# Choosing 16 experts among 96 sums instead of 256, and making the gate rows of four tokens by two operations

## The chip, the cores and the metric

One core of a Trainium2 chip runs the whole program. Its engines work side by side and wait for each other by semaphores: TensorE (PE in the profile; PEld is its weight load), VectorE (DVE), ScalarE (ACT), GpSimd (POOL) and SyncE (SP, which here only issues DMAs). The metric is the time of one execution on the device, in microseconds (us). The kernel before takes 3847.57 us, the median of three runs (3845.66 to 3850.11).

## The reference, cut to what matters

Two layers work on 512 latent and 256 context tokens with 1024 features. Each layer has a mixer and then PEER, a retrieval among 16384 = 128 x 128 experts. For each token and each of 8 heads, PEER takes the 16 best of 128 scores twice, adds every one of the first 16 to every one of the second 16, and takes the 16 best of these 256 sums:

```
sv, si = lax.top_k(s, PEER_TOPK)
cand = (sv[:, :, 0, :, None] + sv[:, :, 1, None, :]).reshape(PEER_BLOCK, PEER_HEADS, kk)
cidx = (si[:, :, 0, :, None] * PEER_NKEYS + si[:, :, 1, None, :]).reshape(PEER_BLOCK, PEER_HEADS, kk)
top_s, pos = lax.top_k(cand, PEER_TOPK)
eidx = jnp.take_along_axis(cidx, pos, axis=-1)
gate = jax.nn.softmax(top_s, axis=-1)
act = jax.nn.gelu(jnp.einsum('nd,nhkd->nhk', hb, u_tab[eidx]).astype(F32), approximate=False)
w = (gate * act).astype(hb.dtype)
return jnp.einsum('nhk,nhkd->nd', w, v_tab[eidx])
```

Both lists of 16 are sorted, largest first. The sum of number a of the first list and number b of the second has at least (a+1)(b+1)-1 others that are no smaller, so it can be among the 16 best only where (a+1)(b+1) is at most 16.

## The kernel before, in words

The time goes to PEER. Tokens come in tiles of 128. In layer 0 tiles 0 to 3 are *dense*: all 16384 experts are computed for them and multiplied by gates that are zero except at the chosen ones. Tiles 4 and 5 are *gathered*: the rows of the chosen experts alone are fetched, one row per token, by indirect DMAs. In layer 1 tiles 0 to 2 are dense and tile 3 is gathered. Each layer has two stages.

- **The u stage.** `u_chunk` loads 128 experts of the table u (`c_raw`), splits them into two parts (`c_hi` by ACT, `c_lo` by DVE, line 298) and multiplies both with the dense tokens: 24 matmuls into `ups`. There are 128 such chunks per layer, and 16 chunks of the query weights of the same form between them. ACT applies the gelu and the result goes to memory.
- **The v stage.** For each chunk POOL multiplies that result with the gates (`w`, line 1059), ACT and DVE split the product and the table v, and PE multiplies them into `res`.

Around the u chunks stands the other work of PEER, which DVE carries above all:

- `scores` takes the 16 best of 128 scores (lines 716 to 721).
- `select` takes the 16 best of the 256 sums: four heads are added at a time (`cand`, line 737), each head is searched by five DVE instructions (lines 743 to 748), the position in the list is taken apart into its two numbers (lines 754 and 756), and the indices are looked up (`eq`, lines 758 to 768).
- `build` makes the gates of a dense tile, 32 steps of four tokens. ACT makes one factor `o1`, of each token (lines 805 and 806). DVE makes the other, `o2`: one instruction per token (line 809) compares a row of 0 to 127 with the token's second index and multiplies by its gate. PE multiplies the two (`gps`), and ACT copies the result to `stage` (line 814).
- `gather` fetches one row per token for one of 128 choices (POOL's indirect DMA, line 667). DVE then makes its product with the token (line 671, table u) or adds it, weighted, to `g_acc` (line 675, table v). A gathered tile has 256 such steps.

A planner sets the order. After each chunk `back` advances three clocks, of PE, DVE and the DMAs, by the costs in `COST`. Pieces of `select` and `build` for the dense tiles are placed evenly over the chunks. While DVE's clock is behind PE's, further pieces of the early work are issued: the choice for the gathered tiles and rows to gather, at 1.15 us each, up to `GU` of them (340 in layer 0, 160 in layer 1). Rows that the u stage did not gather are spread over the v stage. Each engine then runs its instructions in the order so laid down.

Of the kernel before, what the change touches and what calls it, by code (L numbers as in the profile page):

```python
# [9 lines left out]
F32 = mybir.dt.float32  # L10
F32R = mybir.dt.float32r
BF16 = mybir.dt.bfloat16
# [6 lines left out]
P = 128  # L19
# [35 lines left out]
COST = {"build": (1.03, .73, .85), "gather": (1.15, 1.46, 0), "cand": (1.14, 0, 0), "top": (1.0, 0, 0), "top2": (.67, 0, 0),  # L55
# [6 lines left out]
class Tracked:  # L62
    """an engine, with its latest instruction"""
# [13 lines left out]
def kernel(tc, a, out):  # L77
# [52 lines left out]
    class Operand:  # L130
        """The two exact parts of what a phase multiplies with, features on partitions"""

        class Cols:
            """columns in more than one tile"""
# [19 lines left out]
        def fill(self, b, src):  # L154
            """block b of the features"""
            for c0, c1 in self.bounds:
                split(self.hi[:, b, c0:c1], self.lo[:, b, c0:c1], src[:, c0:c1])

        def freed(self):
            """a token tile's room twice in the last columns, which nothing reads any more"""  # L160
            c0, c1 = self.bounds[1]
            return [self.pool.tile([P, KB, c1 - c0], F32, name=f"{self.name}{z}f", tag=f"{self.name}{z}{c0}")[:, :, :P]
                    for z in "hl"]
# [17 lines left out]
    def mod_piece(l, j, w, pp, tag="small", bufs=2, after=None, queue=SP):  # L181
        """512 columns of the modulation, four column groups of the array side by side"""
# [43 lines left out]
    def like(v, shape_of):  # L226
        """a row of features as the blocks that another one comes in"""
        return v if len(shape_of.shape) == len(v.shape) else v.rearrange("p (b n) -> p b n", n=P)

    def resid_norm(y, xsrc, gb, wp, bufs=2, tp=None, tmp=None, xb=2, cut=1):  # L230
        """alpha x + gate y of one token tile, its mean and the inverse of its deviation"""
# [19 lines left out]
    def resid_ln(y, xsrc, dst, gb, lg, lb, wp, xo=None, bufs=2, tp=None, xb=2, cut=1):  # L251
        """LN(alpha x + gate y) of one token tile, in dst"""
# [9 lines left out]
    def normed(y, xsrc, gb, wp, bufs=2, tp=None, tmp=None, xb=2, cut=1):  # L262
        """the same without the gain and the bias of the norm, which what follows applies on its own"""
# [12 lines left out]
    def behind_norm():  # L276
        """what may wait until the latest norm is through"""
# [8 lines left out]
    def fold(i, l, sh, sc):  # L286
        """gain and bias of norm i together with the modulation that follows it"""
# [15 lines left out]
    def mm_chunk(ps, wh, wl, hh, hl, n):  # L303
        """ps[m, tok] = w^T h over the KB blocks of the contraction."""
# [16 lines left out]
    def turn(hf, ps, xt, t, scale, shift, all_act=False, b0=0):  # L321
        """x scale + shift with features on partitions"""
# [17 lines left out]
    def peer_hT(l, t, xt, mod, gt, wp, wide, n):  # L340
        """operand of the PEER sub-layer, in steps; a tile whose experts are gathered keeps it whole, in both layouts"""
# [13 lines left out]
    def proj_rows(l, wp, pp, small):  # L355
        """what proj_out multiplies and adds along the features"""
# [9 lines left out]
    def proj_out(op, l, wh, wl, xsrc, gt, wp, rows, wops, turned, nb, lags):  # L366
        """x <- LN(alpha x + gate * (mix @ w_out)) and what PEER takes of it, in steps; says which tile comes next"""
# [60 lines left out]
    LATE = [(0, 10), (0, 11)] + [(1, j) for j in range(4)]  # L428

    def mixer0(gt):  # L430
        with ExitStack() as es:
# [37 lines left out]
            def taps(g, up):  # L469
                """the taps of one group of channels, by the vector engine or by the scalar engine and GpSimd"""  # L470
# [12 lines left out]
            def taps_pe(g, uh, ul):  # L483
                """the taps of one group of channels, by the tensor engine with diagonal matrices"""
# [112 lines left out]
            # layer norm over the channels, which lie on the partitions  # L597
# [49 lines left out]
    def peer(op, l, gt, xdst):  # L647
# [45 lines left out]
        with ExitStack() as es:  # L693
# [29 lines left out]
            chosen = {}  # L723

            def select(t):
# [6 lines left out]
                sh4 = [P, HB, TOPK, TOPK]  # L732
                ijg = wp.tile([P, 3, HEADS, TOPK], F32, name=f"ijg{z}", bufs=1)
                for h0 in (0, HB):
                    hs = slice(h0, h0 + HB)
                    cand = wp.tile(sh4, F32, name=f"cand{z}", bufs=1)
                    V.tensor_tensor(cand, v4[:, hs, 0, :].unsqueeze(3).to_broadcast(sh4),
                                    v4[:, hs, 1, :].unsqueeze(2).to_broadcast(sh4), op=OP.add)
                    yield "cand"
                    for h in range(HB):  # L740
                        src = cand[:, h].rearrange("p a b -> p (a b)")
                        s2 = wp.tile([P, 256], F32, name=f"c2{z}", bufs=1)
# [8 lines left out]
                    for s in range(2):  # L751
                        pi = wp.tile([P, HB, TOPK], U32, name=f"pi{z}", bufs=2)
                        if s == 0:
                            V.tensor_scalar(pi, pos[:, hs], 4, None, op0=OP.logical_shift_right)
                        else:
                            V.tensor_scalar(pi, pos[:, hs], 15, None, op0=OP.bitwise_and)
# [34 lines left out]
                chosen[t] = tr  # L791
                yield "gates"

            def build(t):
                """the gates of a dense tile, by expert and token"""
                tr = chosen.pop(t)
                W8 = 4
                for g in range(P // TG):
                    stg = wp.tile([P, P, TG], F32, name="stage", bufs=2)
                    for b in range(TG // W8):  # L800
# [6 lines left out]
                        for i in range(W8):  # L807
                            n1 = slice(n0 + i, n0 + i + 1)
                            V.tensor_scalar(o2[:, i], iota, tr[:, 1, n1], tr[:, 2, n1],
                                            op0=OP.is_equal, op1=OP.mult)  # L810
# [7 lines left out]
            def merged(gens):  # L818
                """generators side by side, each as far along as the other; gens: (generator, its cost)"""
# [875 lines left out]
```

## Time and profile before

| | before |
|---|---|
| runs, median (lowest to highest) | 3847.57 us (3845.66 to 3850.11) |
| profiled execution, first to last instruction | 3842.2 us |
| PE busy | 3659.1 us |
| DVE busy | 3152.0 us |
| ACT busy | 1836.8 us |
| POOL busy | 1722.5 us |
| u stage of layer 0, from chunk 17 on | about 447 to 1390 us of the span |
| v stage of layer 0 | about 1390 to 2070 us |
| u stage of layer 1 | about 2525 to 3290 us |
| v stage of layer 1 | about 3290 to 3830 us |

The busy share of PE counts a matmul from its start to a modelled end. Several overlap, so a busy PE can still be slower than it could be. How much work it did is read from the number of matmuls in a stretch. For DVE, an instruction's duration includes some 0.07 us in which the next one already runs, so the engine's busy time is less than the sum of its durations.

### The profile page before, as it was taken

The page shows a single profiled execution, that of the slowest core. Times are in us where ns is not written, and L with a number is a line of the kernel's source. Part 1 is how long each engine was busy: PE and PEld are TensorE (multiplying, and loading weights), DVE is VectorE, ACT ScalarE, POOL GpSimd, SP SyncE. Part 2 cuts the span into 40 slices and gives each one's busy share as a digit, 9 for nine tenths or more (in the row PEclk, how much of TensorE's full clock was granted, in tenths as well). Part 3 has the DMA queues.
Part 4 walks back from the last instruction along what each step waited for, and adds up shares of the span by engine and source line. Part 5 has one row for each costly group of instructions (what it writes and reads, how often), then busy time and mean ns, then how long its engine had stood idle before and what let it go on. Part 6 is the DMA issues. An engine that isn't in the chain of part 4 may idle for free. (4 is left out here: it accounts for less than half of the span.)

```text
span 3842.2 us, 57154 instructions
## 1 busy us (share of the span) xinstructions
PE 3659.1 (95%) x20375; PEld 3162.6 (82%) x20375; DVE 3152.0 (82%) x6412; ACT 1836.8 (48%) x3234; POOL 1722.5 (45%) x1225
## 2 busy tenths in 40 slices
PE   7789999999999999999998999899999999999998
PEld 5567877788888778888887888789999999887876
DVE  4877899999999868998886616688999987688778
ACT  4243322378888832322224424533358988333332
POOL 4300055444445557887871203103422223577764
PEclk9899999999999999999999999899999999999999
DMA  5225598889999999999993330157978989888885
GB/s 232 88 91 198 180 326 307 302 319 355 366 344 356 373 338 355 359 367 367 356 342 136 127 127 4 66 192 276 314 263 320 314 290 342 300 318 321 324 314 197
DMA packets 377149, 1044.00 MB, mean 272 GB/s; under 512 B 32288, under 2 KB 171936, under 8 KB 346656
## 3 DMA queue, kind: packets, MB, share of 16 engines
q1 hardware_dynamic: 262960, 619.56, 44.1%
q0 software_dynamic: 113760, 420.53, 30.4%
q8 instruction: 160, 2.62, 0.3%
q14 instruction: 125, 1.02, 0.1%
q10 hardware_dynamic: 144, 0.26, 0.0%
HBM read 915.98 MB, written 124.26 MB: 271 GB/s over the span
## 5 line engine op out<-in xcount | busy, mean ns | idle before, releaser
L667 POOL DMA_INDIRECT g_row<-in_peer_u_dram,g_idx x384 | 529.1, 1378 | 788.5 <-DVE g_row L671 397.0
L667 POOL DMA_INDIRECT g_row<-in_peer_v_dram,g_idx x384 | 576.5, 1501 | 308.0 <-DVE g_acc L675 188.9
L297 ACT CAST c_hi<-c_raw 128x1024 fp32r<-128x1024 f32 x304 | 318.2, 1047 | 593.3 <-PE ups L69 484.4
L298 DVE TENSOR_TENSOR v_lo<-v_raw,v_hi 128x1024 fp32r<-128x1024 f32 x256 | 409.7, 1600 | 214.8 <-ACT v_hi L297 214.5
L297 ACT CAST v_hi<-v_raw 128x1024 fp32r<-128x1024 f32 x256 | 269.3, 1052 | 656.5 <-DMA v_raw<-in_peer_v_dram 380.0
L1059 POOL TENSOR_TENSOR w<-ag,gg 128x512 f32<-128x512 f32 (+1 forms) x256 | 455.2, 1778 | 278.7 <-DVE w_lo L298 234.2
L69 PE MATMUL res<-v_hi,w_hi 128*128 128x512 f32 x1792 | 556.1, 391 | 12.6 <-ACT w_hi L297 12.6
L69 PE MATMUL res<-v_lo,w_hi 128*128 128x512 f32 x1792 | 555.3, 390 | 1.1
L69 PE MATMUL res<-v_hi,w_lo 128*128 128x512 f32 x1792 | 554.5, 390 | 0.0
L675 DVE SCALAR_TENSOR_TENSOR g_acc<-g_row,g_act,g_acc 128x1024 f32<-128x1024 f32 x381 | 533.2, 1399 | 2.2
L298 DVE TENSOR_TENSOR c_lo<-c_raw,c_hi 128x1024 fp32r<-128x1024 f32 x304 | 373.3, 1229 | 147.0 <-ACT c_hi L297 143.9
L671 DVE SCALAR_TENSOR_TENSOR g_row<-g_row,g_h 128x1024 f32<-128x1024 f32 x384 | 488.1, 1288 | 6.2 <-DMA g_row<-in_peer_u_dram,g_idx 6.0
L69 PE MATMUL ups<-opah,c_hi 128*128 128x512 f32 x1152 | 458.5, 398 | 4.9 <-ACT c_hi L297 4.9
L69 PE MATMUL ups<-opah,c_lo 128*128 128x512 f32 x1152 | 453.4, 394 | 9.7 <-DVE c_lo L298 9.4
L69 PE MATMUL ups<-opal,c_hi 128*128 128x512 f32 x1152 | 451.3, 392 | 0.0
L69 PEld LDWEIGHTS res<-v_hi,w_hi 128*128 128x128 f32 x1792 | 336.6, 188 | 85.9 <-ACT w_hi L297 16.7
L69 PEld LDWEIGHTS res<-v_lo,w_hi 128*128 128x128 f32 x1792 | 336.3, 188 | 75.0 <-DVE v_lo L298 5.6
L69 PE MATMUL ups<-opch,c_hi 128*128 128x384 f32 x1152 | 393.7, 342 | 3.7 <-ACT c_hi L297 3.7
L69 PEld LDWEIGHTS res<-v_hi,w_lo 128*128 128x128 f32 x1792 | 336.2, 188 | 71.1 <-DVE w_lo L298 2.0
L69 PE MATMUL ups<-opch,c_lo 128*128 128x384 f32 x1152 | 387.8, 337 | 3.6 <-DVE c_lo L298 3.6
L69 PE MATMUL ups<-opcl,c_hi 128*128 128x384 f32 x1152 | 386.7, 336 | 0.0
L805 ACT ACTIVATE o<-iota,ijT 128x128 f32<-128x128 f32 x896 | 293.0, 403 | 0.2
(469 smaller groups left out, 6699.8 us busy)
## 6 DMA issues: line engine op xcount, KB each, us to landing
c_raw<-in_uT_dram SPq DMA_DIRECT2D x256, 512.0 KB, 6.1
v_raw<-in_peer_v_dram SPq DMA_DIRECT2D x128, 1024.0 KB, 7.7
G_d<-stage SPq DMA_DIRECT2D x56, 1024.0 KB, 7.8
c_raw<-in_peer_wq_dram SPq DMA_DIRECT2D x64, 512.0 KB, 4.9
gg<-G_d SPq DMA_DIRECT2D x64, 512.0 KB, 9.8
A_d<-at SPq DMA_DIRECT2D x120, 256.0 KB, 6.4
ag<-A_d SPq DMA_DIRECT2D x30, 1024.0 KB, 10.9
gg<-G_d SPq DMA_DIRECT2D x64, 384.0 KB, 8.9
```

Source lines behind the costliest of these rows:

```text
L69: self.last = self.engine.matmul(*args, **kw)
L297: copied[0] = S.copy(hi, src)
L298: return V.tensor_tensor(lo, src, hi.bitcast(F32), op=OP.subtract)
L667: G.indirect_dma_start(out=row, out_offset=None, in_=a[f"peer_{'uv'[tab]}{l}"], in_offset=bass.IndirectOffsetOnAxis(ap=idx[i][:, s:s + 1], ...
L671: V.scalar_tensor_tensor(row, row, 1.0, h, op0=OP.mult, op1=OP.mult, accum_out=w)
L675: V.scalar_tensor_tensor(acc, row, w, acc, op0=OP.mult, op1=OP.add)
L805: S.activation(o1[:, i], iota, AF.Abs, bias=tr[:, 0, n0 + i:n0 + i + 1])
L1059: G.tensor_tensor(w.rearrange("p (t m) -> p t m", m=TG), ag[:, i], gg[:, :, (c + i) % GG, :], op=OP.mult)
```

## The change

The sums that cannot be among the 16 best are left out. `cand` now has 96 places per head, made by three additions: 2 x 16 sums, 2 x 8 and 12 x 4. Each search looks at 96 places. A position no longer splits by a shift and a mask alone, and eight small instructions take it apart where two did. For the gates, the indices of a tile are kept in bf16 as well (`jT`), and `o2` of four tokens is made by two DVE instructions: a comparison of 512 elements in bf16 (`oe`), and a multiplication by the gates that writes 512 elements of 4 bytes. The multiplication runs over the tokens innermost, and the four tokens' rows lie 512 bytes apart in `o2`. So each element is written 512 bytes from the one before it. Three costs in the planner's table are lowered (`cand`, `top`, `top2`); those of `build`, `gather` and `eq` stay. The rest of the diff removes comments, and is left out here.

```diff
-COST = {"build": (1.03, .73, .85), "gather": (1.15, 1.46, 0), "cand": (1.14, 0, 0), "top": (1.0, 0, 0), "top2": (.67, 0, 0),
+COST = {"build": (1.03, .73, .85), "gather": (1.15, 1.46, 0), "cand": (.55, 0, 0), "top": (.7, 0, 0), "top2": (.45, 0, 0),
...
+            CAND = ((0, 0, 2, 16), (32, 2, 2, 8), (48, 4, 12, 4))
+            fifteen = wp.tile([P, TOPK], U32, name="fifteen")
+            V.memset(fifteen, 15)
+            W8 = 4
+            iotar = wp.tile([P, P, W8], BF16, name="iotar")
+            V.tensor_copy(iotar, iota.unsqueeze(2).to_broadcast([P, P, W8]))
...
-                    cand = wp.tile(sh4, F32, name=f"cand{z}", bufs=1)
-                    V.tensor_tensor(cand, v4[:, hs, 0, :].unsqueeze(3).to_broadcast(sh4),
-                                    v4[:, hs, 1, :].unsqueeze(2).to_broadcast(sh4), op=OP.add)
+                    cand = wp.tile([P, HB, 96], F32, name=f"cand{z}", bufs=1)
+                    for p0, a0, na, nb in CAND:
+                        shc = [P, HB, na, nb]
+                        V.tensor_tensor(cand[:, :, p0:p0 + na * nb].rearrange("p h (a b) -> p h a b", b=nb),
+                                        v4[:, hs, 0, a0:a0 + na].unsqueeze(3).to_broadcast(shc),
+                                        v4[:, hs, 1, :nb].unsqueeze(2).to_broadcast(shc), op=OP.add)
...
-                        src = cand[:, h].rearrange("p a b -> p (a b)")
-                        s2 = wp.tile([P, 256], F32, name=f"c2{z}", bufs=1)
+                        src = cand[:, h]
+                        s2 = wp.tile([P, 96], F32, name=f"c2{z}", bufs=1)
...
-                            V.tensor_scalar(pi, pos[:, hs], 4, None, op0=OP.logical_shift_right)
-                        else:
-                            V.tensor_scalar(pi, pos[:, hs], 15, None, op0=OP.bitwise_and)
+                    V.tensor_scalar(pb, pos[:, hs], 32, None, op0=OP.is_ge)
+                    V.scalar_tensor_tensor(pb, pos[:, hs], 48, pb, op0=OP.is_ge, op1=OP.add)
+                    V.tensor_scalar(pa, pb, -1.0, 4.0, op0=OP.mult, op1=OP.add)
+                    V.tensor_tensor(pa, pos[:, hs], pa, op=OP.logical_shift_right)
+                    V.tensor_tensor(pm, fifteen.unsqueeze(1).to_broadcast(sh3), pb, op=OP.logical_shift_right)
+                    V.tensor_tensor(pm, pos[:, hs], pm, op=OP.bitwise_and)
+                    V.scalar_tensor_tensor(pb, pb, 2.0, pb, op0=OP.mult, op1=OP.mult)
+                    V.tensor_tensor(pa, pa, pb, op=OP.subtract)
+                    for pi in (pa, pm):
...
+                jb = wp.tile([P, P], BF16, name="jT", bufs=2)
+                S.copy(jb, pt[:, 1])
...
-                        for i in range(W8):
-                            n1 = slice(n0 + i, n0 + i + 1)
-                            V.tensor_scalar(o2[:, i], iota, tr[:, 1, n1], tr[:, 2, n1],
-                                            op0=OP.is_equal, op1=OP.mult)
+                        sh, nb = [P, P, W8], slice(n0, n0 + W8)
+                        oe = wp.tile(sh, BF16, name="oe", bufs=2)
+                        V.tensor_tensor(oe, iotar, jb[:, nb].unsqueeze(1).to_broadcast(sh), op=OP.is_equal)
+                        V.tensor_tensor(o2.rearrange("p n c -> p c n"), oe, tr[:, 2, nb].unsqueeze(1).to_broadcast(sh),
+                                        op=OP.mult)
```

The first place is DVE's order behind the 106th `c_lo`, in the u stage of layer 0, while the gates of one dense tile are made and the next tile's choice runs. Before it reads so (`o` with its buffer's number is `o2`, one row of four instructions per step; x4 and x2 are counts):

```order
L298 TENSOR_TENSOR c_lo<-c_raw,c_hi 128x1024
L675 SCALAR_TENSOR_TENSOR g_acc<-g_row,g_act,g_acc 128x1024
L743 MAX topd<-candd 128x8
L675 SCALAR_TENSOR_TENSOR g_acc<-g_row,g_act,g_acc 128x1024
L744 MAX_INDEX posd<-topd,candd 128x8
L745 MATCH_REPLACE c2d<-topd,candd 128x256
L809 TENSOR_SCALAR o_9167<-iota,ijT 128x128 x4
L809 TENSOR_SCALAR o_9184<-iota,ijT 128x128 x4
L675 SCALAR_TENSOR_TENSOR g_acc<-g_row,g_act,g_acc 128x1024
```

And now, behind the same `c_lo` (`oe` and `o` are the two operations of a step):

```order
L298 TENSOR_TENSOR c_lo<-c_raw,c_hi 128x1024
L824 TENSOR_TENSOR oe<-iotar,jT 128x512
L757 MAX topd<-c2d 128x8
L825 TENSOR_TENSOR o_9222<-oe,ijT 128x128x4
L758 MAX_INDEX posd<-topd,c2d 128x8
L824 TENSOR_TENSOR oe<-iotar,jT 128x512
L675 SCALAR_TENSOR_TENSOR g_acc<-g_row,g_act,g_acc 128x1024 x3
```

Before, each gate step is one run of four instructions. Now its two operations stand apart with other work between them, and the second operation of the last step shown comes only behind the next `c_lo`. Three gathered rows stand in both pieces. The second place is POOL's queue where the u stage of layer 0 ends and the products of the v stage (`w`) begin, before:

```order
L667 DMA g_row<-in_peer_u_dram,g_idx_2679 128x1024 x128
L667 DMA g_row<-in_peer_v_dram,g_idx_2679 128x1024 x128
L667 DMA g_row<-in_peer_u_dram,g_idx_2680 128x1024 x67
L1059 TENSOR_TENSOR w<-ag,gg 128x512 x3
L667 DMA g_row<-in_peer_u_dram,g_idx_2680 128x1024
```

And now:

```order
L667 DMA g_row<-in_peer_u_dram,g_idx_2679 128x1024 x128
L667 DMA g_row<-in_peer_v_dram,g_idx_2679 128x1024 x128
L667 DMA g_row<-in_peer_u_dram,g_idx_2680 128x1024 x95
L1075 TENSOR_TENSOR w<-ag,gg 128x512 x3
L667 DMA g_row<-in_peer_u_dram,g_idx_2680 128x1024
```

So 28 gathered rows move from the v stage into the u stage of layer 0 (323 stood ahead of the first `w`, now 351), and 6 in layer 1. Counted along DVE's order between the same `c_lo` (the numbers of the chunks run through the program), with the time at which that part ran before:

| chunks | time before, us | gathered rows, before / now | gate steps, before / now | heads searched, before / now |
|---|---|---|---|---|
| 17 to 77, layer 0 | 447 to 818 | 122 / 135 | 6 / 5 | 21 / 18.5 |
| 77 to 137, layer 0 | 818 to 1238 | 147 / 162 | 93 / 92.5 | 22.5 / 22 |
| 137 to 153, layer 0 | 1238 to 1364 | 44 / 44 | 29 / 30 | 0 / 0 |
| 221 to 277, layer 1 | 2833 to 3122 | 63 / 71 | 62 / 59 | 17 / 17 |
| 277 to 301, layer 1 | 3122 to 3266 | 33 / 22 | 34 / 37 | 0 / 0 |

## Rows read from the trace of the kernel before

**Rows 1.** Busy time by stretch: us, each engine's busy (x), granted clock, DMA

```profile
core 0: us, PE busy (x) PEld busy (x) DVE busy (x) ACT busy (x) POOL busy (x), PEclk, DMA share, GB/s
447.00:744.00 297.00, 284.74 (x1284) 229.62 (x1283) 289.84 (x926) 85.67 (x108) 145.12 (x106) 0.99 0.82 296
818.00:1238.00 420.00, 415.34 (x2195) 354.50 (x2194) 415.91 (x883) 351.56 (x698) 206.01 (x148) 1.00 0.97 357
1400.00:2060.00 660.00, 660.00 (x2914) 546.64 (x2913) 563.82 (x530) 197.72 (x251) 509.96 (x311) 1.00 0.91 343
2833.00:3122.00 289.00, 289.00 (x1841) 288.51 (x1840) 261.50 (x641) 256.56 (x501) 75.09 (x63) 1.00 0.88 308
3122.00:3266.00 144.00, 137.17 (x855) 132.45 (x854) 108.70 (x216) 125.47 (x258) 46.48 (x33) 0.99 0.90 317
1238.00:1338.00 100.00, 93.01 (x517) 77.05 (x516) 91.00 (x209) 95.22 (x202) 57.60 (x39) 1.00 0.99 367
```

**Rows 2.** The same stretch of layer 0, matmuls of ups, then of gps

```profile
818.00:1238.00 420.00, 345.06 (x1444) 266.04 (x1442) 35.57 (x61) 1.00 0.97 357
818.00:1238.00 420.00, 93.36 (x742) 92.02 (x743) 97.46 (x92) 1.00 0.97 357
```

**Rows 3.** The chain of waits: start us, us, what

```profile
2868.28 1.78 PE gps L69 x16
```

**Rows 4.** Waits, 420 to 800 us, then 1238 to 1338: us in total, times, longest

```profile
PEld ups L69 <- DVE c_lo L298: 13.8, 14, 5.9
PEld gps L69 <- ACT o L806: 12.9, 14, 1.3
```

**Rows 5.** DVE in order of time from 818 us: start, us, what

```profile
824.19 1.22 DVE L298 TENSOR_TENSOR c_lo<-c_raw,c_hi 128x1024 fp32r<-128x1024 f32 x1
825.33 1.11 DVE L809 TENSOR_SCALAR o<-iota,ijT 128x128 f32<-128x128 f32 x4
826.35 0.42 DVE L747 MAX8 topd<-c2d 128x8 f32<-128x256 f32 x1
```

**Rows 6.** DVE by line, 818 to 1238 us: xcount | busy us, mean ns | idle

```profile
L675 DVE SCALAR_TENSOR_TENSOR g_acc<-g_row,g_act,g_acc 128x1024 f32<-128x1024 f32 x127 | 163.0, 1283 | 0.1
L809 DVE TENSOR_SCALAR o<-iota,ijT 128x128 f32<-128x128 f32 x372 | 107.0, 365 | 0.0
L743 DVE MAX8 topd<-candd 128x8 f32<-128x256 f32 x22 | 9.4, 426 | 0.0
L737 DVE TENSOR_TENSOR candd<-sv 128x1024 f32<-128x1024 f32 x5 | 6.1, 1226 | 0.0
L754 DVE TENSOR_SCALAR pid<-posd 128x64 uint32<-128x64 uint32 x6 | 1.3, 213 | 0.0
```

**Rows 7.** The whole span by line and shape: DVE, then ACT

```profile
L716 DVE MAX8 sv<-scps 128x8 f32<-128x128 f32 x160 | 47.0, 294 | 17.4 <-PE scps L69 17.1
L1251 DVE TENSOR_TENSOR ML<-mB,mx 128x4 f32<-128x4 f32 x12 | 1.7, 159 | 0.0
L1171 DVE TENSOR_TENSOR rny<-rny,rope 128x128 f32<-128x128 f32 x4 | 1.2, 289 | 0.6 <-POOL rsw L1169 0.6
L298 DVE TENSOR_TENSOR opal<-csq,opah 128x512 fp32r<-128x512 f32 x4 | 2.8, 691 | 3.1 <-ACT opah L297 3.0
L766 DVE TENSOR_TENSOR eqd<-eqd 128x512 bf16<-128x512 bf16 x28 | 11.8, 424 | 0.1
L768 DVE TENSOR_TENSOR ijgd<-eqd 128x64 f32<-128x64 bf16 x28 | 7.9, 286 | 0.1
L814 ACT COPY stage<-gps 128x512 f32<-128x512 f32 x224 | 237.1, 1069 | 0.7
L212 ACT COPY gb<-gps 128x512 f32<-128x512 f32 x6 | 3.5, 585 | 8.5 <-PE gps L69 8.5
```

**Rows 8.** DVE by line, 2833 to 3122 us: the gate rows and a gathered row

```profile
L671 DVE SCALAR_TENSOR_TENSOR g_row<-g_row,g_h 128x1024 f32<-128x1024 f32 x63 | 76.2, 1215 | 0.0
L809 DVE TENSOR_SCALAR o<-iota,ijT 128x128 f32<-128x128 f32 x248 | 69.1, 348 | 0.5 <-PE gps L69 0.5
```

More of the change, by code (lines that the diff above doesn't have):

```diff
@@ L732, in select @@
                 sh4 = [P, HB, TOPK, TOPK]
+                sh3 = [P, HB, TOPK]
                 ijg = wp.tile([P, 3, HEADS, TOPK], F32, name=f"ijg{z}", bufs=1)
@@ L750, in select @@
                     eqs = []
-                    for s in range(2):
-                        pi = wp.tile([P, HB, TOPK], U32, name=f"pi{z}", bufs=2)
-                        if s == 0:
-                            V.tensor_scalar(pi, pos[:, hs], 4, None, op0=OP.logical_shift_right)
-                        else:
-                            V.tensor_scalar(pi, pos[:, hs], 15, None, op0=OP.bitwise_and)
+                    pb, pa, pm = (wp.tile(sh3, U32, name=f"p{y}{z}", bufs=2) for y in "bam")
+                    V.tensor_scalar(pb, pos[:, hs], 32, None, op0=OP.is_ge)
[7 more added lines that the diff above has]
+                    for pi in (pa, pm):
                         eq = wp.tile(sh4, BF16, name=f"eq{z}", bufs=2)
@@ L790, in select @@
                 S.copy(tr, pt)
-                chosen[t] = tr
+                jb = wp.tile([P, P], BF16, name="jT", bufs=2)
+                S.copy(jb, pt[:, 1])
+                chosen[t] = tr, jb
                 yield "gates"
             def build(t):
-                tr = chosen.pop(t)
-                W8 = 4
+                tr, jb = chosen.pop(t)
                 for g in range(P // TG):
```

## The prediction

> **What bounds the kernel now.** I read the busy times by stretch first, then DVE's groups by line inside the stretches that the change touches, then the waits, and last the durations of like instructions over the whole span.
>
> By stretch, PE looks full everywhere, so the reader is to count matmuls instead. In the v stage of layer 0 PE is busy for all of 660 us and starts 2914 matmuls of 512 columns, 0.2265 us each [rows 1]. That is PE's full rate, since the granted clock is 1.00. In the stretch 818 to 1238 us there are 1444 matmuls of `ups` at that rate, 327 us, and 742 of `gps` [rows 2], which run 16 in 1.78 us where PE is the chain [rows 3], so 82 us more. PE needs 409 of the 420 us. DVE is busy for 415.9 of the same 420 us [rows 1]. So DVE sets this stretch, with PE 11 us behind as the next bound. From 447 to 744 us it is DVE too (289.8 of 297), and there PE does wait for `c_lo` [rows 4]. In layer 1, from 2833 to 3122 us, PE has no idle time and DVE is busy for 261.5 of 289, so 27.5 us are free on it [rows 1]. At the ends of both u stages, where gate steps come without a choice beside them, ACT is the fullest engine (95.2 of 100 us from 1238 to 1338) and PE waits for ACT's factor [rows 1, 4]. So the change is decided on DVE, stretch by stretch, by what goes and what comes.
>
> **What one piece costs.** An instruction's start to the next one's start is about 0.07 us less than its duration: a `c_lo` of 1.22 us is followed after 1.14, four gate rows of 1.11 after 1.02 [rows 5]. I take 0.07 off everything.
>
> *A gate step before:* 372 instructions, 93 steps, take 107.0 us [rows 6], so 1.15 a step, 1.08 net.
>
> *A gate step now,* first operation: 512 elements, all bf16. The nearest row is an addition of 512 bf16 elements at 424 ns; the dearest that it could be is 691, as 512 elements of 4 bytes take [rows 7]. I take 0.42, as the type is the same. Second operation: 512 elements with a result of 4 bytes, so 691 ns at least. But each element is written 512 bytes from the last one. No DVE row of before writes so. ACT's copy to `stage` writes 512 elements 64 bytes apart and takes 1069 ns; its copy of the same size from the same kind of tile to neighbouring places takes 585 [rows 7]: 0.94 ns more for each element. And DVE has one instruction that reads its 64 elements 32 bytes apart (line 768): 286 ns, where 4 elements take 159 and 128 take 289, so that 64 should take about 222 [rows 7]: 1.0 ns more for each. Both say that an element on a place of its own costs about one more nanosecond. For 512 that is 0.53 us, and 691 becomes about 1.22 us. The bounds are 0.69 (nothing more) and 1.26 (ACT's ratio 1.83). I take 1.22, since both rows with such a step show it. A step is then 0.42 + 1.22 - 0.14 = 1.50 us net, 0.42 more than before.
>
> The Trainium skill describes how such places are read (Advanced Engine Details and Errata, SBUF Cachelines): accesses that each fall in another line of 16 bytes are slowed, and two in a line are needed for full speed. It names no price; the two rows agree with it. Against it stands another page (VectorE: DVE Perf Modes, Mode 1x (REGULAR) — the baseline), by which this mode makes one result a cycle, odd strides included. By the first the sum below stands, by the second it is that of the first rival.
>
> *A searched head:* five instructions over 256 elements at about 426 ns become five over 96. 128 elements take 294 [rows 6, 7], so 96 should take 0.26, an estimate by the slope between the two. That saves 0.16 each, 0.8 us a head. *The additions:* one of 1226 ns becomes three of 128, 64 and 192 elements, 0.29 + 0.22 + 0.36 by the rows at 4 and 128 elements [rows 6, 7], 0.5 us less net for four heads. *The positions:* eight instructions where two were. At 213 ns each [rows 6] that is 0.14 net, 0.8 us more for four heads; zero to 0.3 each would make 0 to 2 us of it. *A gathered row:* 1.283 us with table v [rows 6], 1.215 with table u [rows 8], 1.21 and 1.15 net. ACT's extra copy of the indices, seven in all, and the two constants made once are nothing beside this: ACT is busy for 1837 of 3842 us.
>
> **The sum.** The planner does not keep what the choice saves. It charges less for a choice, finds its DVE clock behind PE's sooner, and puts gathered rows there: 28 in layer 0 and 6 in layer 1 move ahead, with their DMAs on POOL's queue.
>
> - 447 to 818 us: 13 rows more (+15), 18.5 searched heads cheaper (-15) and 2.5 fewer (-5), additions and positions about +1, one gate step fewer but five dearer (+1). I take -3.
> - 818 to 1238 us: 93 gate steps (+39), 15 rows (+18), 22 heads (-18), five additions (-2.5), six times the positions (+5). Sum +42. DVE has 4 us left that are waits, and PE's 11 us are already inside the 420, so all of it is on the path: +42.
> - 1238 to 1364 us: 30 steps (+13) and as many rows as before. ACT is the bound, but in its first 100 us DVE has 91 busy and would have 103. I take +5.
> - 2833 to 3122 us: a step was 69.1/62 - 0.07 = 1.05 us net [rows 8], so 59 steps at 1.50 make +24; 8 rows (+9), 17 heads (-14), additions and positions +2. DVE rises by 21 to 283 of 289. PE's chunks hide most of it; for the crowding I take +3, and 0 to 10 as bounds.
> - 3122 to 3266 us: 37 steps in place of 34 (+20), 11 rows fewer (-13); DVE 116 of 144 with ACT in front. +2.
> - v stages: 28 and 6 rows fewer to add up. In layer 0 PE is full for all 660 us, so nothing comes back; layer 1 has too few rows to matter. 0. This is the point of the case: rows are moved from where DVE's work was free to where it is the bound.
>
> Together +49. The profiled execution spans 3842.2 us, the median of the runs is 3847.57, so 5.4 us lie around the span or between executions. The span becomes 3891 and the time about 3897 us.
>
> **The rivals.**
>
> *The write is not slowed* (second operation 0.69 us). A step is 0.97 net, 0.11 less than before. Then 818 to 1238 us gets -7 in all, the first stretch -3, the ends about -1: 3837 us. For it speaks that no DVE row writes with such a step; against it, both rows that have one. PE's floor of 409 us forbids more than -11 there. This is the case on the faster side, and it decides for any second operation below about 0.75 us.
>
> *The same, but the DMAs eat it.* In that stretch the queues are busy 0.97 at 357 GB/s [rows 1], and 15 rows of 512 KB are 7.9 MB, 5% of what it moves. If it gets no longer, `c_raw` comes late by about what is won: 3847 us, no change.
>
> *Half the price.* The write costs about 0.95 us: 0.27 less a step, -25 in the second stretch and -3 around it: 3870 us. For it speaks only that DVE's one row is a read with two such inputs.
>
> *The comparison runs at one element a cycle* (0.69 us). 0.27 more a step: +25, then +8 at the end of layer 0, and in layer 1 DVE passes PE (283 + 16 of 289), +10 and +3: about 3943 us. Against it, the bf16 addition of as many elements takes 424 ns [rows 7].
>
> *The choice saves nothing*, since the planner refills it: that is not a rival but part of the sum, and the rows counted in the order show it.
>
> **How the numbers follow.** The forecast (3880 to 3925) has 0.63, half the price (3855 to 3880) 0.12, the slow comparison (3925 to 3955) 0.10, no change 0.07, faster 0.08. The predicted time is the forecast's, 3897. The range that leaves two in ten out is 3858 to 3935: outside lie no change, faster and about half of the slow comparison. The likeliest case alone has 3880 to 3925. A measurement of this kernel tells about 0.2%, 7.7 us, from no change. By that, slower has 0.85, no change 0.07 and faster 0.08.
>
> **What would show it.** In the profile after: the second operation of a gate step near 1.22 us and the comparison near 0.42; a search of 96 places near 0.26; DVE busy all through the u stage of layer 0, which ends some 45 us later, and PE waiting for `c_lo` between 818 and 1238 us of before, with fewer matmuls in 100 us; the v stage of layer 0 as long as before. It is wrong if the second operation takes about 0.7 us, or if that stretch gets no longer although DVE has more to do in it.

## The result: slower, by half of what was forecast

| | before | after |
|---|---|---|
| runs on one chip, median (lowest to highest) | 3850.11 us (3845.66 to 3855.41), 5 runs | 3873.78 us (3862.14 to 3875.51), 5 runs |
| profiled execution, first to last instruction | 3842.2 us | 3873.7 us |
| ratio of the times, 95% interval | 1 | 1.0056 [1.0041, 1.0071] |

The changed kernel is 0.56% slower, 24 us, where 49 were forecast. The time lies in the range that was given, and the direction is right; but it lies below the likeliest case (3880 to 3925), within the bounds of the rival at half the price. The two spans differ by 31.5 us, more than the medians. The profiled execution of after took 3875.51 us, 1.8 us more than its span and the slowest of its five. With the same 1.8 us the one of before took about 3844, below all of its runs. So between stretches of the two traces some 5 to 8 us in all are scatter.

The busy times of after by stretch, cut at the same `c_lo` as those of before [rows 1] (whose first row ends earlier, at 744 us); the columns are stretch, length, each engine's busy time and instructions, granted clock, DMA share and GB/s:

```profile
core 0: us, PE busy (x) PEld busy (x) DVE busy (x) ACT busy (x) POOL busy (x), PEclk, DMA share, GB/s
446.00:819.00 373.00, 359.03 (x1614) 290.99 (x1613) 360.12 (x1142) 124.41 (x173) 197.94 (x140) 0.98 0.86 312
819.00:1261.00 442.00, 421.32 (x2184) 354.91 (x2182) 437.38 (x775) 354.80 (x703) 267.45 (x162) 0.99 0.97 354
1261.00:1392.00 131.00, 122.30 (x654) 102.65 (x654) 109.09 (x167) 104.73 (x215) 65.79 (x46) 1.00 1.00 370
1423.00:2083.00 660.00, 660.00 (x2913) 546.69 (x2912) 499.96 (x477) 196.61 (x250) 471.55 (x284) 1.00 0.89 324
2868.00:3156.00 288.00, 286.57 (x1816) 285.70 (x1815) 273.36 (x568) 250.41 (x488) 99.39 (x72) 1.00 0.90 322
3156.00:3303.00 147.00, 139.45 (x887) 135.13 (x886) 105.69 (x127) 133.34 (x277) 34.54 (x23) 1.00 0.82 289
```

The second row carries the result. The same 60 chunks took 420 us before and take 442, with as many matmuls (2184, 2195 before), and DVE is busy for 437 of the 442. Of the other stretches the end of that stage got 5 us longer (131 against 126 from 1238 to 1364 us of before), the first one 2 (373 against 371), layer 1's last 3. In 660 us of the v stage of layer 0 PE starts as many matmuls as before (2913, 2914 before), while DVE's busy time there fell from 564 to 500 us: the rows that left it gave nothing back. From the first matmul of `res` to the last that stage takes 711 us, and took 710.

The ends of these stretches are starts of `c_lo` on DVE, which can run ahead of PE. Counted on PE instead, from the start of one matmul of `ups` to the start of another, the same two in both kernels, the busy stretch takes 420 us before and 448 after, and the end of that stage 126 and 124. So the two together got 25 to 27 us longer, and how this splits between them depends on where the border is set.

DVE by line in the stretch 819 to 1261 us of after, to be laid beside [rows 6]; behind the count stand busy us, mean ns, and idle time:

```profile
L675 DVE SCALAR_TENSOR_TENSOR g_acc<-g_row,g_act,g_acc 128x1024 f32<-128x1024 f32 x121 | 154.3, 1275 | 2.7 <-DMA g_row<-in_peer_v_dram,g_idx 1.8
L825 DVE TENSOR_TENSOR o<-oe,ijT 128x512 f32<-128x512 bf16 x92 | 98.4, 1083 | 0.0
...
L671 DVE SCALAR_TENSOR_TENSOR g_row<-g_row,g_h 128x1024 f32<-128x1024 f32 x41 | 48.9, 1222 | 1.7 <-DMA g_row<-in_peer_u_dram,g_idx 1.7
L824 DVE TENSOR_TENSOR oe<-iotar,jT 128x512 bf16<-128x512 bf16 x93 | 37.5, 415 | 0.0
...
L753 DVE MAX8 topd<-candd 128x8 f32<-128x96 f32 x22 | 5.4, 245 | 0.0
...
L746 DVE TENSOR_TENSOR candd<-sv 128x128 f32<-128x128 f32 (+2 forms) x15 | 3.8, 288 | 0.0
```

The comparison (L824) takes 0.415 us and a search 0.245, as forecast. The second operation (L825) takes 1.083, where 1.22 was taken. There are 162 rows in place of 147, as counted in the order. How much of the 1.08 us the engine is really held shows in DVE's order of time (start us, us, what):

```profile
899.72 1.07 DVE L825 TENSOR_TENSOR o<-oe,ijT 128x512 f32<-128x512 bf16 x1
900.63 1.21 DVE L298 TENSOR_TENSOR c_lo<-c_raw,c_hi 128x1024 fp32r<-128x1024 f32 x1
901.77 0.40 DVE L824 TENSOR_TENSOR oe<-iotar,jT 128x512 bf16<-128x512 bf16 x1
902.10 0.24 DVE L757 MAX8 topd<-c2d 128x8 f32<-128x96 f32 x1
902.27 1.10 DVE L825 TENSOR_TENSOR o<-oe,ijT 128x512 f32<-128x512 bf16 x1
903.22 0.06 DVE L758 MATCH_VALUE_LOAD posd<-topd,c2d 128x8 f32 x1
```

From the start of an L825 to the start of the next instruction it is 0.91 and 0.95 us here, and 0.92 in the mean of the whole span. Behind `c_lo` the overlap is 0.07 (901.77 less 900.63 is 1.14 of 1.21, and 0.08 in the mean); behind L825 it is 0.15 to 0.17. So a gate step holds DVE for 0.33 + 0.92 = 1.25 us. Four gate rows before held it for 1.02 [rows 5]. The step costs 0.23 us more, not 0.42.

The longest waits of PE's weight loads in that stretch of after (us in total, times, longest):

```profile
PEld gps L69 <- ACT o L821: 14.8, 10, 2.9
PEld ups L69 <- DVE c_lo L298: 7.6, 8, 2.2
```

And in that of before:

```profile
PEld gps L69 <- ACT o L806: 5.8, 6, 1.5
PEld ups L69 <- DVE c_lo L298: 2.7, 5, 1.0
```

PE does run into DVE there, as forecast, but the wait for `c_lo` grew by 5 us alone. The wait for ACT's factor grew by 9, though ACT is busy no longer than before (355 us, 352 before). That both come from the second operation is seen below, where it writes in a row. How DVE holds up ACT's factor these rows don't tell, and some 8 of the 22 us show as no wait here.

### The profile page after: what moved, and what is told of

Same layout as the page of the kernel before. It is cut to its first block, busy times and chain, and to the rows that moved or that the text cites. A ratio compares the mean times of both kernels' runs of the same rounds, so it can differ in the third digit from the quotient of the medians.

```text
span 3873.7 us, 56946 instructions
## 1 busy us (share of the span) xinstructions
PE 3669.3 (95%) x20375; PEld 3169.8 (82%) x20375; DVE 3109.4 (80%) x6128; ACT 1839.1 (47%) x3241; POOL 1785.7 (46%) x1225
## 5 line engine op out<-in xcount | busy, mean ns | idle before, releaser
L667 POOL DMA_INDIRECT g_row<-in_peer_u_dram,g_idx x384 | 562.7, 1465 | 670.7 <-DVE g_row L671 296.4
L1075 POOL TENSOR_TENSOR w<-ag,gg 128x512 f32<-128x512 f32 (+1 forms) x256 | 487.8, 1906 | 379.6 <-DVE w_lo L298 286.3
L298 DVE TENSOR_TENSOR v_lo<-v_raw,v_hi 128x1024 fp32r<-128x1024 f32 x256 | 392.4, 1533 | 286.9 <-ACT v_hi L297 286.9
L675 DVE SCALAR_TENSOR_TENSOR g_acc<-g_row,g_act,g_acc 128x1024 f32<-128x1024 f32 x381 | 520.1, 1365 | 4.4 <-DMA g_row<-in_peer_v_dram,g_idx 1.8
L671 DVE SCALAR_TENSOR_TENSOR g_row<-g_row,g_h 128x1024 f32<-128x1024 f32 x384 | 471.7, 1245 | 12.6 <-DMA g_row<-in_peer_u_dram,g_idx 12.6
```

The costliest lines, as they stand in the source:

```text
L298: return V.tensor_tensor(lo, src, hi.bitcast(F32), op=OP.subtract)
L667: G.indirect_dma_start(out=row, out_offset=None, in_=a[f"peer_{'uv'[tab]}{l}"], in_offset=bass.IndirectOffsetOnAxis(ap=idx[i][:, s:s + 1], ...
L671: V.scalar_tensor_tensor(row, row, 1.0, h, op0=OP.mult, op1=OP.mult, accum_out=w)
L675: V.scalar_tensor_tensor(acc, row, w, acc, op0=OP.mult, op1=OP.add)
L1075: G.tensor_tensor(w.rearrange("p (t m) -> p t m", m=TG), ag[:, i], gg[:, :, (c + i) % GG, :], op=OP.mult)
```

## The experiments

Times are medians, and ratios are against runs of the kernel before on the same chip. "The busy stretch" is the one from chunk 77 to chunk 137 (420 us before, 442 after). A and B are the theory and the rival that each expectation names; the theory behind them all is that DVE is the bound there and that its second operation pays for each element that lies apart.

**The gate rows of before, everything else of after.** The two operations are undone; the new choice, its costs and the 34 moved rows stay.

```diff
-                        V.tensor_tensor(oe, iotar, jb[:, nb].unsqueeze(1).to_broadcast(sh), op=OP.is_equal)
-                        V.tensor_tensor(o2.rearrange("p n c -> p c n"), oe, ...)
+                        for i in range(W8):
+                            V.tensor_scalar(o2[:, i], iota, tr[:, 1, n1], tr[:, 2, n1], op0=OP.is_equal, op1=OP.mult)
```

> The changed kernel with the gate rows made as before (four instructions a step); the choice among 96 sums, the lowered costs and so the 34 rows moved ahead stay. Theory A (the gate step is what costs): a step falls from 1.32 to 1.06 us net between the 77th and 137th chunk, so DVE there from 437 to about 413 us, and the stretch from 442 to about 419; with 5 us at the end of layer 0's u stage and 3 in layer 1 the time is about 3845 us, no slower than before. Rival B (the rows moved ahead are what costs): the time stays near 3870 us.

Measured 3842.69 us (3836.95 to 3848.60), ratio 0.9989 [0.9978, 1.0000]. The busy stretch is 424 us. So the gate rows are what makes the change slow: 26 us beside after by the ratios, 31 by the medians. And the new choice alone, with its refill by the planner, wins hardly anything.

**The second operation writes its results in a row.** It does the same work, and its 512 results go to neighbouring places, so that the gates stand in the wrong order.

```diff
-V.tensor_tensor(o2.rearrange("p n c -> p c n"), oe,
+V.tensor_tensor(o2.rearrange("p n c -> p (n c)").rearrange("p (c n) -> p c n", n=W8), oe,
```

> The changed kernel with the second operation of a gate step writing its 512 elements to neighbouring places; the gates then stand in the wrong order, with as many instructions and bytes as before on every engine. Theory A (places 512 bytes apart make that write slow): the operation falls from 1.09 to about 0.69 us, the stretch of chunks 77 to 137 meets PE's floor at about 412 us, and the time is about 3838 us. Rival B (it is slow for its mix of a bf16 and a 4-byte input): it stays near 1.09 us and the time near 3870.

Measured 3844.00 us (3840.92 to 3847.99), ratio 0.9992 [0.9983, 1.0001]. DVE's gate operations in it, whole span:

```profile
L825 DVE TENSOR_TENSOR o<-oe,ijT 128x512 f32<-128x512 bf16 x224 | 152.0, 686 | 25.9 <-PE gps L69 25.8
...
L824 DVE TENSOR_TENSOR oe<-iotar,jT 128x512 bf16<-128x512 bf16 x224 | 89.7, 417 | 0.3 <-ACT jT L806 0.2
```

The same two lines of after, whole span:

```profile
L825 DVE TENSOR_TENSOR o<-oe,ijT 128x512 f32<-128x512 bf16 x224 | 240.2, 1089 | 13.2 <-PE gps L69 13.0
...
L824 DVE TENSOR_TENSOR oe<-iotar,jT 128x512 bf16<-128x512 bf16 x224 | 89.3, 416 | 0.3 <-ACT jT L806 0.2
```

With nothing changed but where the results go, 1089 ns become 686, and the kernel gains 25 us by the ratios, 30 by the medians. The write's places are the cause. The two waits of PE's weight loads, in this kernel's busy stretch (823 to 1241 us), fall back with it:

```profile
PEld gps L69 <- ACT o L821: 6.4, 8, 1.7
PEld ups L69 <- DVE c_lo L298: 0.4, 1, 0.4
```

A step now holds DVE for 0.94 us from start to start, 0.09 less than four old gate rows, which is 8 us in 93 steps. The busy stretch is 418 us where the experiment before has 424, but the whole time is the same within 1.3 us. It missed the 3838 expected by 6, and where the rest went isn't shown.

**The old costs in the planner.** `cand`, `top` and `top2` are charged as before, so that no rows move.

```diff
-"cand": (.55, 0, 0), "top": (.7, 0, 0), "top2": (.45, 0, 0)
+"cand": (1.14, 0, 0), "top": (1.0, 0, 0), "top2": (.67, 0, 0)
```

> The changed kernel with the planner's old costs for cand, top and top2, so that the 34 rows stay in the v stages as before. Theory A (the refill costs its full DVE time, since DVE is the bound of the u stage of layer 0 and PE that of the v stage): 13 rows fewer before chunk 77 and 15 fewer up to chunk 137 give back about 15 and 18 us, some of it only down to PE's floor, and the v stage gets no longer: about 3845 us. Rival B (a row costs in the v stage what it costs in the u stage): about 3870 us, as now.

Measured 3854.70 us (3847.79 to 3860.40), ratio 1.0015 [1.0003, 1.0028]. The expectation of 3845 is missed by 10 us. The stretch before the busy one fell to 363 us, 9 less where 15 were expected. The busy one is 432 us by the starts of `c_lo`; counted on PE it fell from 448 to 431, nearly the 18 us expected. The rest of the miss isn't explained.

**The new choice alone.** Old gate rows and old costs, the edits of the first and the third experiment together.

```diff
-"cand": (.55, 0, 0), "top": (.7, 0, 0), "top2": (.45, 0, 0)
+"cand": (1.14, 0, 0), "top": (1.0, 0, 0), "top2": (.67, 0, 0)
...
-                        V.tensor_tensor(o2.rearrange("p n c -> p c n"), oe, ...)
+                            V.tensor_scalar(o2[:, i], iota, tr[:, 1, n1], tr[:, 2, n1], op0=OP.is_equal, op1=OP.mult)
```

> The choice among 96 sums alone: gate rows as before, and the old costs, so that no row moves. Theory A: DVE loses about 19 us between chunks 77 and 137, where PE's floor of 409 us lets about 8 of them count, and 15 us before chunk 77, where all count: about 3827 us. Rival B (PE is the bound and DVE only looks busy): 3847 us, no change.

Measured 3835.88 us (3827.49 to 3843.92), ratio 0.9967 [0.9955, 0.9979]: 12 us faster than before, where some 20 were expected. The busy stretch of this kernel:

```profile
811.50:1221.20 409.70, 408.78 (x2171) 351.15 (x2171) 400.76 (x919) 349.11 (x686) 205.63 (x146) 1.00 0.97 361
```

PE is busy for 409 of 410 us, and DVE for 401. That is near the 409 us that the prediction worked out for PE, but the row holds 2171 matmuls where before has 2195 [rows 1]; counted on PE, for the same matmuls, the stretch takes 414 us. So the choice's saving is real, and it ends at PE's floor, 6 us below the old length by this count and 10 by the starts of `c_lo`. The stretch before it gave some 9 us (362 us, 371 before), where 15 were expected. With the two experiments before it makes a square, in us beside before (ratio times 3850): choice and old costs -13, and with the refill -4; new gates too and old costs +6, and with the refill +22 (24 by the medians). The gate operations cost 19 us without the refill and 26 to 31 with it, the refill 8 with the old gates and 16 to 19 with the new. Each ratio is known to some 5 us, so that the two costs of the refill are hardly apart by the whole times alone.

**The price by itself.** In front of the program stand six groups of four DVE multiplications of 512 elements. The first five write with steps of 4, 8, 16, 64 bytes and in the gate rows' form; the sixth reads with a step of 64 bytes. It is one run, read for these durations alone.

```diff
+        def step(t, s):
+            return t[:, :512 * s].rearrange("p (n s) -> p n s", s=s)[:, :, 0]
...
+        for _ in range(4):
+            V.tensor_tensor(step(dst, 4), srb, src, op=OP.mult)
```

> The changed kernel with 24 DVE multiplications put in front of its work: 512 elements, one bf16 and one 4-byte input, four times each with a result whose places lie 4, 8, 16 and 64 bytes apart, four times written as the gate rows are (tokens innermost, 512 bytes apart), and four times read 64 bytes apart and written in a row. Only the durations count here. Theory A (an element on a place of its own costs more, whatever the distance): 4 and 8 bytes take 0.69 us, 16 and 64 bytes and the gate rows' form one and the same, near 1.09 or 1.22. Rival B (the distance counts): the time grows from 8 to 16, 64 and 512 bytes.

DVE by line, dearest group first (count, busy us, mean ns, idle). The steps of lines 148, 150, 152 and 154 are 4, 8, 16 and 64 bytes; 156 is the gate rows' form, and 158 the read:

```profile
L152 DVE TENSOR_TENSOR prdst<-prsrb,prsrc 128x512 f32<-128x512 bf16 x4 | 4.3, 1082 | 0.1
...
L156 DVE TENSOR_TENSOR prdst<-prsrb,prsrc 128x512 f32<-128x512 bf16 x4 | 4.2, 1045 | 0.1
...
L154 DVE TENSOR_TENSOR prdst<-prsrb,prsrc 128x512 f32<-128x512 bf16 x4 | 4.1, 1023 | 0.1
L158 DVE TENSOR_TENSOR prsrc<-prdst,prsrc 128x512 f32<-128x512 f32 x4 | 4.1, 1017 | 0.1
...
L150 DVE TENSOR_TENSOR prdst<-prsrb,prsrc 128x512 f32<-128x512 bf16 x4 | 2.8, 694 | 0.1
...
L148 DVE TENSOR_TENSOR prdst<-prsrb,prsrc 128x512 f32<-128x512 bf16 x4 | 2.8, 691 | 0.1
```

Two elements in 16 bytes cost nothing (694 against 691), one in 16 bytes costs 0.39 us, and a longer step costs no more than that. This is 0.65 to 0.76 ns an element, and not the 0.94 to 1.0 ns of ACT's copy and of the read at line 768 [rows 7]. That difference is the forecast's error in the duration; why those two rows pay more isn't shown. The Trainium skill's rule (Advanced Engine Details and Errata, SBUF Cachelines) puts the border at lines of 16 bytes that want two accesses each; the trace agrees, with the numbers above. The Trainium skill's rule that was weighed against it (VectorE: DVE Perf Modes, Mode 1x (REGULAR) — the baseline), one result a cycle in a mode that takes odd strides too, does not hold here: 1.02 to 1.08 us against 0.69.

**Let PE read apart instead.** DVE writes the gates in a row with the tokens innermost, and PE's moving operand is read 16 bytes apart. The result is the same.

```diff
-o2 = wp.tile([P, W8, P], F32, name="o2", bufs=2)
+o2 = wp.tile([P, P, W8], F32, name="o2", bufs=2)
...
-PE.matmul(pg[:, i], o1[:, i], o2[:, i], ...)
+PE.matmul(pg[:, i], o1[:, i], o2[:, :, i], ...)
```

> The changed kernel with the gate rows kept as the second operation makes them, tokens innermost, so that DVE writes in a row and PE reads its 128 columns 16 bytes apart. Theory A: DVE's operation takes 0.69 us; if PE reads at full rate (gps stays at 16 in 1.78 us) the time is about 3844 us. Rival B (PE pays for what DVE saves): gps takes longer, and as PE is the next bound with 11 us to spare in the stretch of chunks 77 to 137 and 742 of these matmuls in it, each 0.05 us more there costs some 25 us: 3870 us or more.

Measured 4029.30 us (4023.36 to 4034.23), ratio 1.0454 [1.0440, 1.0468]. Its chain of waits in layer 1 (start us, us, what), to be read beside [rows 3]:

```profile
2981.04 4.17 PE ups L69 x24
2985.21 3.63 PE gps L69 x16
2988.84 4.17 PE ups L69 x24
```

Sixteen `gps` take 3.63 us where 1.78 were needed. Times 1792 matmuls that is 207 us more on PE; some 155 of them came out beside after, some 180 beside the run that writes in a row. The engine that pays decides: PE was 6 to 11 us behind the bound, and it cannot take what DVE was relieved of.

**Tokens outermost.** Both operations run over the 128 places innermost, so that the results are written in a row in the right order; the token's index and its gate are repeated 128 times.

```diff
-sh = [P, P, W8]
+sh = [P, W8, P]
...
-V.tensor_tensor(oe, iotar, jb[:, nb].unsqueeze(1).to_broadcast(sh), op=OP.is_equal)
+V.tensor_tensor(oe, iotab.unsqueeze(1).to_broadcast(sh), jb[:, nb].unsqueeze(2).to_broadcast(sh), op=OP.is_equal)
```

> The changed kernel with the two operations of a gate step run over tokens outermost: each token's row is written in a row, the token's index and gate are the operand repeated 128 times, and the result is the one that PE reads as before. Theory A (the places of the result are what made the second operation slow): it takes 0.69 us; if the comparison stays near 0.42 the time is that of the write in a row, about 3843 us. Rival B: the comparison, with an operand repeated innermost, falls back to one element a cycle, 0.69 us, so that a step costs 0.27 more than that: about 3862 us.

Measured 3870.28 us (3866.05 to 3874.27), ratio 1.0049 [1.0036, 1.0061], not told apart from after. Its two operations:

```profile
L825 DVE TENSOR_TENSOR o<-oe,ijT 128x512 f32<-128x512 bf16 x224 | 152.6, 687 | 20.6 <-PE gps L69 20.2 <-DVE posd L758 0.2
L824 DVE TENSOR_TENSOR oe<-iotab,jT 128x512 bf16<-128x512 bf16 x224 | 149.6, 683 | 0.2 <-ACT jT L806 0.2
```

The multiplication became cheap and the comparison dear: 416 ns became 683 when one of its bf16 inputs is a value repeated innermost. By these durations this is rival B; the time is 8 us above its 3862. The Trainium skill (VectorE: DVE Perf Modes, Mode 2×_1P — pack two bf16 into one 32-bit read) wants neighbouring elements for two results a cycle; a repeated value has none, and the trace agrees. So with this layout of `o2` the gates of four tokens have one dear operation either way.

**Charge the scores what they take.** On the new choice alone, the scores of layer 0 are charged 1.25 in place of 1.05 us, so that fewer rows fill the first stretch.

```diff
-back(mmt + 0.25 * nd, 1.15 + 1.05 * nd, 1.46)
+back(mmt + 0.25 * nd, 1.15 + (1.25 if l == 0 else 1.05) * nd, 1.46)
```

> The choice among 96 sums alone with the old costs, and the planner charging 1.25 instead of 1.05 us per tile for the scores of layer 0, as they really take (39.2 us for 8 x 4 tiles): 11 rows fewer before chunk 77, which go to the v stage. Theory A (DVE is the bound there by what the planner does not see, and rows are free in the v stage): the stretch 17 to 77 falls from 361 to about 350 us, PE's floor being some 340, and the time to about 3826 us. Rival B: the v stage takes the rows back at their price, 3836 us.

Measured 3832.99 us (3829.83 to 3845.09), ratio 0.9952 [0.9937, 0.9966]. This is the fastest kernel here, faster than both; beside the new choice alone the intervals overlap. The reason given for it failed: 11 rows left the stretch before the busy one, but that still takes 362 us, not 350:

```profile
447.50:809.70 362.20, 356.09 (x1624) 290.32 (x1623) 337.89 (x1138) 126.96 (x179) 156.63 (x116) 1.00 0.81 287
```

DVE is busy for 338 of 362 us and is no longer the bound. PE shows 356 busy, and whether that is its floor or many short waits isn't told by these rows: what holds this stretch then stays open.

**Charge gathered rows more.** On the new choice alone, a row of layer 0 is charged 1.40 in place of 1.15 us; 258 rows then stand ahead of the v stage, where before had 323.

```diff
                 dve, dma, pe = COST[kind]
+                dve += .25 * (kind == "gather" and l == 0)
```

> The choice among 96 sums alone with the old costs, and a gathered row of layer 0 charged 1.40 instead of 1.15 us: 22 rows fewer before chunk 77, 26 fewer up to 137, 7 fewer after, 55 more in the v stage of layer 0. Theory A: the stretch 17 to 77 falls to PE's floor of about 342 us (from 361), the next one cannot fall (it is at its floor of 409), the v stage of layer 0 stays at 830 us up to the first normal chunk of layer 1, as it did with 28 rows more or fewer: about 3817 us. Rival B (with 254 rows the v stage meets POOL or DVE, 510 and 564 of 660 us busy before): it grows by 10 us or more and the time stays above 3828.

Measured 3874.61 us (3870.54 to 3881.68), ratio 1.0059 [1.0046, 1.0072]. Theory A fell here. The busy stretch kept its 408 us, though DVE has far less to do in it:

```profile
808.00:1216.00 408.00, 406.76 (x2159) 348.67 (x2158) 371.65 (x899) 348.39 (x686) 166.75 (x122) 1.00 0.91 330
```

DVE is busy for 372 of the 408 us and the queues 0.91 (0.97 with the new choice alone), so it is PE that holds this stretch here. But the v stage of layer 0 and what follows it, 830 us to the next layer before, took 873. Its window, and its longest waits there (us in total, times, longest):

```profile
1400.00:2060.00 660.00, 640.29 (x2743) 517.72 (x2742) 604.66 (x598) 184.28 (x232) 543.73 (x349) 0.98 0.98 373
```

```profile
ACT v_hi L297 <- DMA v_raw<-in_peer_v_dram: 256.4, 52, 16.1
ACT w_hi L297 <- POOL w L1071: 182.9, 71, 5.8
...
PEld res L69 <- ACT w_hi L297: 20.7, 11, 4.5
```

The same view of before reads 138.3 and 54.2 us for the first two, and has no wait of PE:

```profile
ACT v_hi L297 <- DMA v_raw<-in_peer_v_dram: 138.3, 26, 13.7
...
ACT w_hi L297 <- POOL w L1059: 54.2, 27, 3.5
```

With 254 rows left for it in place of 189, the queues of the v stage are 0.98 busy at 373 GB/s (0.91 at 343 before [rows 1]), `v_raw` and POOL's products come late, and PE starts 2743 matmuls in 660 us, not 2914. PE itself waits longest for `w_hi`, which waits for POOL's `w`; whether the DMA queues or POOL, which also issues the gathered rows, set the pace isn't separated by this run. DVE is busy for 605 of the 660 us. So the prediction's sentence that DVE's work was free in the v stage holds for taking 28 rows out; putting 65 in is not free, and the price need not be DVE's.

**Tokens outermost, with the costs of the fastest kernel.**

```diff
-"cand": (.55, 0, 0), "top": (.7, 0, 0), "top2": (.45, 0, 0)
+"cand": (1.14, 0, 0), "top": (1.0, 0, 0), "top2": (.67, 0, 0)
-back(mmt + 0.25 * nd, 1.15 + 1.05 * nd, 1.46)
+back(mmt + 0.25 * nd, 1.15 + (1.25 if l == 0 else 1.05) * nd, 1.46)
```

> The same gate steps (tokens outermost) together with the planner's old costs and 1.25 us per tile for the scores of layer 0, so that 11 rows move to the v stage instead of 28 out of it. Theory A: with a comparison of 0.42 us a step costs DVE 0.95 us where four instructions cost 1.03, and the stretch of chunks 77 to 137 stays at PE's floor of 409 us: as fast as the choice alone with these costs, about 3832 us. Rival B (comparison of 0.69 us): about 3842 us.

Measured 3847.79 us (3836.56 to 3854.23), ratio 0.9990 [0.9979, 1.0001], with 681 and 686 ns for the two operations: B again by the durations, and 6 us above its 3842. With the same costs the old gate rows are 0.4% faster. In no layout tried here with the gates in their right order did the two operations beat the four.

## Why the direction was right and the size was wrong

**What bounds the kernel: right.** DVE set the busy stretch (437 of 442 us busy), with PE behind it as the next bound. PE's floor of 409 was worked out a little low: counted on PE, the runs in which DVE is no longer full take 414 and 415 us.

**The second operation of a gate step: the step that failed.** The sum took 1.22 us for it, 0.07 of that beside the next instruction, and so +0.42 us a step. It takes 1.08 to 1.09, and the next instruction starts after 0.92. Both errors point the same way: the duration was 0.13 too long, because the price per element was taken from ACT and from a read with two such inputs, and not from a DVE write; and the overlap of 0.07 was taken over from instructions of another kind, where 0.15 to 0.17 stands behind this one. A smaller error went the other way: four old rows were taken at 1.08 us, though they hold the engine for 1.02 by [rows 5]. The step is +0.23, so that 93 steps make 21 us and not 39. With that the prediction's own sum for the busy stretch, 18 for rows, 18 and 2.5 saved on the choice, 5 for positions, gives +24; it grew by 22 by the starts of `c_lo`, and by 27 counted on PE.

**The mechanism: right.** Written in a row, the operation takes 686 ns and 25 to 30 us go; by itself it shows the border between 8 and 16 bytes. The rival "the write is not slowed" is out, by 1089 ns. The rival "the comparison runs at one element a cycle" is out for this layout (416 ns), and came true in the other one (683). "Half the price", 0.95 us and 3870, was the nearest in time: its hold on the engine, 0.95 less 0.07, is close to the 0.92 measured, but by luck: its duration is 0.13 too short and its overlap 0.1 too small.

**The planner takes what the choice saves: right.** 34 rows moved as counted in the order. The refill costs 8 us with the old gate rows. With the new ones it costs 16 to 19. That fits a floor of PE that covers part of it with the old rows and little with the new: counted on PE, the refill makes the busy stretch 11 us longer with the old rows (414 to 425) and 17 with the new (431 to 448).

**The other stretches.** The end of the u stage of layer 0 was forecast at +5: it got 5 us longer by the starts of `c_lo` and 2 shorter counted on PE, so that this term isn't settled. The v stages gave nothing back, as forecast. The first stretch was forecast at -3 and came out at +2, layer 1's two at +5 and came out at -1 and +3; the part between the layers, which the change hardly touches, was 5 us longer (389 against 384), and runs of this study have it anywhere from 384 to 389; the part behind the u stage of layer 1 was 5 us shorter (571 against 576). These are within the scatter, and single profiles don't settle them.

## What to carry to other kernels

Fewer instructions is no saving on the engine that bounds a stretch until the layout of the result is priced: write along the innermost dimension, or at least two 4-byte elements in 16 bytes, and check that the new layout doesn't send the cost to another operand or to the engine that reads it. Price an operation by what it holds, from its start to the start of the next one, taken behind an instruction of that same kind. And where a planner refills what is saved, a saving on the bound has to be kept from it: the half of this change that was worth having gains 0.3% with the old costs and 0.1% with the new.

## What was not expected of the hardware

- A DVE write with each 4-byte element in 16 bytes of its own takes 1.02 to 1.08 us for 512 elements in place of 0.69, at 16 bytes as at 64 and 512, and a read with a step of 64 bytes as much (1.02). It is no doubling, and it doesn't grow with distance.
- Behind such a write the next DVE instruction starts 0.15 to 0.17 us before its recorded end, behind others 0.07 to 0.1.
- PE pays more for such a layout than DVE: 16 matmuls with 128 columns of 4 bytes that stand 16 bytes apart take 3.63 us in place of 1.78. That is 0.93 us for the eight of a gate step, where DVE's slow write costs 0.40.
- A bf16 operation of 512 elements goes from 0.416 to 0.683 us when one input is repeated innermost; repeated in an outer dimension it costs nothing (0.416 beside 0.424 for an addition of as many [rows 7]).
